# Transformer layer on one core: x's loads and the six-ahead weight pieces of the output projection begin earlier

## The chip, the cores and the metric

The kernel runs on one core of a Trainium2 chip. The metric is the device time of one execution in microseconds (us), as the median of several runs. Profiles and times by line come from one profiled execution.

## What is computed

The reference is one layer with sliding-window attention, for 512 tokens of width 2048, in float32:

```python
hn = rmsnorm(x, norm_g[0])
y = swa_mixer(hn, swa_w_in[0], swa_w_out[0], swa_sinks[0], rel_bias)   # attention, gated, times w_out
x = x + y
emb = p[0] @ ple_proj[0]
g = jax.nn.sigmoid(rmsnorm(x, ple_norm[0]) @ ple_gate[0])
x = x + emb * g
return rmsnorm(x, final_g)
```

The case is about the last product of `swa_mixer`, `(out * silu(gate)) @ w_out`, a 512 x 2048 by 2048 x 2048 product called the output projection here, and about `x + y`.

## The kernel before

**Stages.** The kernel projects x to queries, keys, values and gates, with the attention woven in (to about 452 us of the profile), then does the output projection, then the gate product with `ple_gate`, and at the end the last norm and the stores.

**Products in three.** Each float32 operand is split into a high and a low part, and TensorE makes three matmuls of one product (`mm3`, L123 to L128): high by high, high by low, low by high. ScalarE casts a raw weight piece to its high part (L700, named `bhi`); VectorE subtracts to get the low part (L701, `blo`).

**The output projection.** It is done as a Strassen scheme of seven half-size products with one of them replaced by smaller ones; the big products come in the order `ORDER_OUT = (1, 7, 6, 5, 3, 4)` (L623). Each has two halves `jj`, and each half four weight pieces `m` of 128 x 1024 float32, 512 KB. One piece feeds twelve matmuls of 128 x 512 in `unit` (L936 to L951). So product 1 has the pieces 0 to 7 of the stage, product 7 the pieces 8 to 15, product 6 the pieces 16 to 23. Smaller products' pieces come between those of the products 5, 3 and 4.

**Pieces and their rooms.** The class `Pieces` (L666 to L735) loads and splits them. `get(i)` is called ahead of piece i's matmuls and calls `ahead(i)` (L714 to L723), which issues the loads of pieces up to i+3, or up to i+6 for pieces between `far_from` and `far_to`, and then the splits up to piece i+2. A raw piece lies in one of three rooms (tag `wraw`, L692) or, between `far_from` and `far_to`, in one of eight (tag `grown`, L688). The eight rooms, like x's, lie in the pool `late` (L907), which takes the space of pools that the projections and the attention used and that are closed before the stage. The high and low parts have three rooms each. Before, `far_from` is the first piece of product 6, piece 16 (L778).

**x.** x is loaded in four parts of 512 columns, 1 MB each (`load_x`, L954 and L955), named by j. The finished sums of each product are added to or taken from x on VectorE (`add_to_x`, L989 to L997). `x_at` (L1070) says after which piece's matmuls a part's load stands in the program: the key is (product, half, piece). The sums of product 1's first half are held back until the first half of product 7, those of its second half until the first half of product 6 (`waiting`, L1071).

**Order on the engines.** In this stage TensorE's and SyncE's instructions keep the order of the program (`manual_schedule`, L63). All loads of pieces and of x are issued by SyncE, in one queue in that order: an instruction that waits for its room holds back all those behind it. The order of VectorE, ScalarE and POOL in this stage is chosen by the framework's planner by its own costs, from what is ready; in the attention and from the gate product's second Strassen product on it is written by hand as well.

Of the kernel before, what the change touches and what calls it, by code (L numbers as in the profile page):

```python
# [55 lines left out]
def trunk_kernel(ctx: ExitStack, tc: tile.TileContext, a: dict):  # L56
# [566 lines left out]
    ORDER_OUT, ORDER_PLE = (1, 7, 6, 5, 3, 4), (2, 7, 1, 6, 5, 3, 4)  # L623
# [115 lines left out]
    def add_stage(nm, order):  # L739
        at = {}  # L740

        def add_embeds(p, jj):
            if nm == "ple_gate" and p in (1, 5, 3, 4):
                j = jj + 2 * (p in (5, 3))
                B.add("proj", a["ple_proj"].rearrange("(k p) d -> p k d", p=P)[:, :, j * 512 : (j + 1) * 512])

        for p in order:
            for jj in range(2):
                if nm == "ple_gate" and (p, jj) == (4, 0):
                    for v in range(2):  # L750
                        at["e", v] = len(B.specs)
                        add_embeds(p, v)
                at[p, jj] = []
                for m in range(4):
                    at[p, jj].append(len(B.specs))
                    if (nm, p) in SUMS:
                        src = summed[nm, p, jj, m]
                    else:
                        src = block(nm, *{1: (1, 1), 2: (2, 1), 3: (2, 2), 6: (1, 1), 4: (2, 1)}[p], jj, m)
                    growing = () if nm == "w_out" else (7, 6, 4)  # L760
                    kind = "one" if p not in growing else "seed" if p == growing[0] else "grow"
                    B.add(kind, src, (nm, jj, m) if p in growing else None)
                    q = SMALL.get((p, jj), {}).get(m) if nm == "w_out" else None
                    if q is not None:
                        v = at.setdefault(("small", q), [])
                        src = summed.get(("small", q, len(v)))
                        if src is None:
                            src = small_block(*{1: (1, 1), 2: (2, 1), 3: (2, 2)}[q], len(v))
                        v.append(len(B.specs))
                        B.add("one", src)  # L770
                if p != 4:
                    add_embeds(p, jj)
        return at

    at_out = add_stage("w_out", ORDER_OUT)
    at_ple = add_stage("ple_gate", ORDER_PLE)

    far_from, far_to = at_out[6, 0][0], at_ple[ORDER_PLE[0], 0][0]  # L778

    class Forms:  # L780

# [285 lines left out]

    turns = []

    x_at = {(1, 1, 1): 0, (7, 0, 0): 2, (7, 0, 3): 1, (7, 1, 1): 3}  # L1070
    waiting = {(7, 0): (1, 0), (6, 0): (1, 1)}  # L1071
    held = {}
    for n, p in enumerate(ORDER_OUT):
# [344 lines left out]
```

## Time and profile before

| | us |
|---|---|
| median of 3 runs | 795.78 |
| the three runs | 794.87, 795.78, 796.67 |
| profiled execution | 794.62 |
| its span, first to last instruction | 792.9 |
| TensorE busy in the span | 782.9 |
| VectorE busy | 600.3 |
| ScalarE busy | 507.1 |
| output projection begins (first matmul with `bhi`) | 451.76 |

A row of a timeline has the start, the duration, the engine (PE is TensorE, DVE VectorE, ACT ScalarE, POOL GpSimd, SP SyncE, whose queue of instructions is SPq), the line, the operation and, in brackets, the idle time before it and what ended it. A row of waits has who waited, for whom, the sum in us, how often, and the longest. A row of the table by stretch has the stretch, its length, each engine's busy time (PE, PEld, DVE, ACT, POOL) with its count of instructions, the granted TensorE clock, the share of the DMA engines that was busy, and GB/s. A row of a load has its size and the median time from issue to landing.

### The profile page before, as it was taken

To read this page: it belongs to the slowest core of one execution; us is meant where nothing else is said; L and a number is where in the kernel's file an instruction comes from. 1 tells how busy PE (TensorE), PEld (TensorE's weight loads), DVE (VectorE), ACT (ScalarE), POOL (GpSimd) and SP (SyncE) were. 2 spreads that over 40 slices of the span, in tenths; PEclk is the share of its full clock that TensorE was granted. 3 is DMA by queue.
4 is the path that set the end of the run, shared out by engine and by line. 5 is a ranking of instruction groups with operands and counts; after the bars stand their busy time and mean duration, and the time that the engine had idled before them with its cause. 6 is when DMAs were issued, how large, how long until landed. Compare 5 with 4: busy or idle time off the path is not lost.

```text
span 792.9 us, 11070 instructions
## 1 busy us (share of the span) xinstructions
PE 782.9 (99%) x3746; PEld 655.1 (83%) x3746; DVE 600.3 (76%) x1043; ACT 507.1 (64%) x1066; POOL 122.2 (15%) x246
## 2 busy tenths in 40 slices
PE   9999999999999999999999999999999999999995
PEld 8888888888888888888888888888888888888885
DVE  4546697877878687877777899778867757988896
ACT  6742576666767586666666654466698656656765
POOL 0020223131323213132222100000000120200000
PEclk9999999999999999999999999999999999999998
DMA  9883499899999989998997369767764995787633
GB/s 352 281 212 132 116 271 316 243 277 235 278 257 267 250 254 272 228 280 238 260 259 187 107 236 393 300 210 235 275 236 140 347 206 195 160 226 216 182 107 106
DMA packets 45577, 185.22 MB, mean 234 GB/s; under 512 B 6656, under 2 KB 7680, under 8 KB 40400
## 3 DMA queue, kind: packets, MB, share of 16 engines
q1 hardware_dynamic: 37984, 145.40, 52.2%
q0 software_dynamic: 7536, 39.12, 26.1%
q8 instruction: 29, 0.48, 0.3%
q14 instruction: 28, 0.23, 0.1%
HBM read 177.63 MB, written 62.97 MB: 303 GB/s over the span
## 4 chain that ended last, share of the span: by engine, by line
PE 91%; DVE 4%; DMA 2%; ACT 1%; issue 1%; ACTq 0%; SPq 0%; DVEq 0%
PE qps L126 7%; PE qps L128 7%; PE qps L127 7%; PE gps L126 7%; PE gps L128 7%; PE gps L127 7%; PE g L126 5%; PE g L127 5%; PE g L128 5%; PE o L127 4%; PE o L126 4%; PE o L128 4%; PE s L462 2%; PE vps L279 2%; DVE blo L701 2%; PE o L557 2%
## 5 line engine op out<-in xcount | busy, mean ns | idle before, releaser
L701 DVE TENSOR_TENSOR blo<-braw,bhi 128x1024 fp32r<-128x1024 f32 x102 | 124.3, 1221 | 40.9 <-ACT bhi L700 40.6
L700 ACT CAST bhi<-braw 128x1024 fp32r<-128x1024 f32 x102 | 107.1, 1051 | 70.0 <-PE o L128 23.6
L126 PE MATMUL gps<-xh,whi 128*128 128x512 f32 x256 | 99.8, 390 | 0.1
L128 PE MATMUL gps<-xh,wlo 128*128 128x512 f32 x256 | 99.9, 390 | 0.0
L127 PE MATMUL gps<-xl,whi 128*128 128x512 f32 x256 | 99.8, 390 | 0.0
L126 PE MATMUL qps<-xh,whi 128*128 128x512 f32 x224 | 87.7, 391 | 0.0
L128 PE MATMUL qps<-xh,wlo 128*128 128x512 f32 x224 | 87.5, 390 | 0.0
L127 PE MATMUL qps<-xl,whi 128*128 128x512 f32 x224 | 87.3, 390 | 0.0
L110 DVE TENSOR_TENSOR wlo<-wraw,whi 128x1024 fp32r<-128x1024 f32 x60 | 73.8, 1232 | 2.9 <-ACT whi L109 2.5
L126 PE MATMUL g<-bhi,fhg 128*128 128x512 f32 x192 | 75.1, 391 | 0.0
L127 PE MATMUL o<-blo,fho 128*128 128x512 f32 x192 | 74.8, 390 | 0.2 <-DVE blo L701 0.2
L126 PE MATMUL o<-bhi,fho 128*128 128x512 f32 x192 | 74.8, 390 | 0.0
L128 PE MATMUL g<-bhi,flg 128*128 128x512 f32 x192 | 74.8, 389 | 0.0
L128 PE MATMUL o<-bhi,flo 128*128 128x512 f32 x192 | 74.7, 389 | 0.0
L127 PE MATMUL g<-blo,fhg 128*128 128x512 f32 x192 | 74.7, 389 | 0.0
L531 POOL TENSOR_SCALAR_AFFINE_SELECT own<-r 64x512 fp32r<-64x512 f32 (+1 forms) x48 | 32.5, 677 | 245.6 <-DVE r L521 245.6
L520 ACT CAST r<-pt 128x256 fp32r<-128x256 f32 x64 | 23.8, 371 | 71.7 <-PE pt L515 71.3
L521 DVE TENSOR_TENSOR r<-pt,r 128x256 fp32r<-128x256 f32 x64 | 27.1, 424 | 55.8 <-ACT r L520 54.9
L109 ACT CAST whi<-wraw 128x1024 fp32r<-128x1024 f32 x60 | 62.3, 1040 | 5.4 <-issue 3.9
L128 PEld LDWEIGHTS gps<-xh,wlo 128*128 128x128 f32 x256 | 48.0, 188 | 10.1
L126 PEld LDWEIGHTS gps<-xh,whi 128*128 128x128 f32 x256 | 48.1, 188 | 9.4 <-PE vps L279 0.5
L495 ACT ACTIVATE t<-t,sm 128x129 f32<-128x129 f32 x128 | 50.6, 397 | 8.0 <-DVE sm L491 6.4
(224 smaller groups left out, 1740.8 us busy)
## 6 DMA issues: line engine op xcount, KB each, us to landing
wraw<-in_w_gate_in SPq DMA_DIRECT2D x32, 512.0 KB, 6.9
w_out<-in_w_out POOLq DMA_DIRECT2D x32, 512.0 KB, 8.6
braw<-w_out SPq DMA_DIRECT2D x32, 512.0 KB, 4.6
wraw<-in_w_q SPq DMA_DIRECT2D x28, 512.0 KB, 6.3
braw<-in_ple_gate SPq DMA_DIRECT2D x24, 512.0 KB, 3.4
braw<-in_w_out SPq DMA_DIRECT2D x22, 512.0 KB, 4.3
xw<-in_first SPq DMA_DIRECT2D x14, 640.5 KB, 6.3
w_out<-in_w_out SPq DMA_DIRECT2D x16, 512.0 KB, 8.5
```

The source lines that it names most:

```text
L109: nc.scalar.copy(hi, raw)
L110: nc.vector.tensor_sub(lo, raw, hi.bitcast(F32))
L126: nc.tensor.matmul(ps, sh, mh, start=first, stop=False, skip_group_check=more)
L127: nc.tensor.matmul(ps, sh, ml, start=False, stop=False, skip_group_check=more)
L128: nc.tensor.matmul(ps, sl, mh, start=False, stop=last, skip_group_check=more)
L279: nc.tensor.matmul(v_ps[t], h[:, c], both[:, :, 256:512], start=f, stop=e, skip_group_check=True)
L495: nc.scalar.activation(su, su, AF.Exp, bias=sm[:, u : u + 1], accum_out=sm[:, 2 + u : 3 + u])
L520: nc.scalar.copy(rh, src)
L521: nc.vector.tensor_sub(rl, src, rh.bitcast(F32))
L531: nc.gpsimd.affine_select(out=flat(own), in_=flat(r).bitcast(F32), pattern=[[0, 8], [sign, HB]], compare_op=ALU.is_ge, fill=0.0, base=-HB ...
L700: nc.scalar.copy(hi, raw)
L701: nc.vector.tensor_sub(lo, raw, hi.bitcast(F32))
```

## The change

Two tables are changed, and nothing else. The first moves the point from which raw pieces use the eight rooms and are issued up to six pieces ahead, from piece 16 to piece 10 (the third piece of product 7's first half). The second moves x's four loads to earlier places in the program: part 0 from behind piece 5's matmuls to behind piece 3's, part 2 from 8 to 5, part 1 from 11 to 7, part 3 from 13 to 9.

```diff
-    far_from, far_to = at_out[6, 0][0], at_ple[ORDER_PLE[0], 0][0]
+    far_from, far_to = at_out[7, 0][2], at_ple[ORDER_PLE[0], 0][0]
...
-    x_at = {(1, 1, 1): 0, (7, 0, 0): 2, (7, 0, 3): 1, (7, 1, 1): 3}
+    x_at = {(1, 0, 3): 0, (1, 1, 1): 2, (1, 1, 3): 1, (7, 0, 1): 3}
```

With it the loads of the pieces 10 and on stand in the program ahead of those of 8 and 9: at piece 4 the program issues 7 and 10, at piece 5 it issues 8 and 11, at piece 6 it issues 9 and 12.

## The prediction

> **What bounds the kernel now.** First the page's engine line, then TensorE's waits.
>
> ```profile
> PE 782.9 (99%) x3746; PEld 655.1 (83%) x3746; DVE 600.3 (76%) x1043; ACT 507.1 (64%) x1066; POOL 122.2 (15%) x246
> PE o L127 <- DVE blo L701: 0.2, 1, 0.2
> ```
>
> TensorE works for 99% of the span, and after its start it waits for a semaphore once, in the output projection, for the low part of a weight piece. What an edit of the loads can win here is that stop; what it can lose is open. The pitch of the matmuls tells the stop's size better than the wait does, since ends are modelled.
>
> ```profile
> 451.76 0.40 PE L126 MATMUL o<-bhi,fho 128*128 128x512 f32 x1
> ...
> 492.14 0.39 PE L127 MATMUL o<-blo,fho 128*128 128x512 f32 x1
> 492.36 0.39 PE L128 MATMUL o<-bhi,flo 128*128 128x512 f32 x1
> 492.59 0.39 PE L126 MATMUL o<-bhi,fho 128*128 128x512 f32 x1
> 493.14 0.50 PE L127 MATMUL o<-blo,fho 128*128 128x512 f32 x1 [0.16 <-DVE blo L701]
> 493.48 0.40 PE L128 MATMUL o<-bhi,flo 128*128 128x512 f32 x1
> ```
>
> Matmuls start 0.227 us apart; twelve make a piece, 2.72 us. Two steps here are longer: 0.55 and 0.34 us, so 0.32 + 0.11 = **0.43 us** are lost. Piece 0 starts at 451.76, so 492.59 = 451.76 + 15 x 2.72 is the start of piece 15 (pieces are numbered from the projection's first). The chain of waits says why it was late:
>
> ```profile
> 483.02 7.68 DMA braw<-w_out
> 490.77 1.06 ACT bhi L700
> 491.86 1.24 DVE blo L701
> 493.14 0.50 PE o L127
> ```
>
> Its load left SyncE at 483.02 and took 7.68 us, then cast, subtraction, matmul. Why 7.68: SyncE's instructions in order, and the busy shares by stretch (the last two columns are DMA share and GB/s).
>
> ```profile
> 458.91 2.06 SPq L693 DMA_DIRECT2D braw<-in_w_out  x2
> 463.52 0.33 SPq L693 DMA_DIRECT2D braw<-w_out  x1
> 463.89 0.43 SPq L955 DMA_DIRECT2D x1s<-in_x  x1
> 466.92 6.60 SPq L693 DMA_DIRECT2D braw<-w_out  x3
> 473.57 0.43 SPq L955 DMA_DIRECT2D x1s<-in_x  x1
> 475.54 6.54 SPq L693 DMA_DIRECT2D braw<-w_out  x5
> 482.13 0.43 SPq L955 DMA_DIRECT2D x1s<-in_x  x1
> 483.02 1.39 SPq L693 DMA_DIRECT2D braw<-w_out  x3
> 484.46 0.44 SPq L955 DMA_DIRECT2D x1s<-in_x  x1
> 459.00:463.50 4.50, 4.50 (x21) 3.72 (x21) 4.50 (x6) 1.69 (x2) 0.00 (x0) 1.00 0.68 228
> 463.50:475.00 11.50, 11.50 (x53) 9.51 (x52) 10.52 (x12) 6.53 (x9) 0.00 (x0) 1.00 0.67 248
> 475.00:505.00 30.00, 29.84 (x132) 24.40 (x131) 26.00 (x31) 13.78 (x16) 0.00 (x0) 1.00 1.01 397
> 490.00:500.00 10.00, 9.84 (x44) 7.83 (x43) 8.97 (x12) 6.57 (x8) 0.00 (x0) 1.00 1.03 417
> 480.00:485.00 5.00, 5.00 (x24) 4.14 (x23) 3.61 (x5) 2.11 (x2) 0.00 (x0) 1.00 0.99 373
> ```
>
> The pieces by these rows, with the code's order: 6 and 7 (from 458.91), 8 (463.52), x0, 9, 10, 11, x2, then 12, 13, 16, 14, 17, then x1, 15, 18, 19, x3. From 475 to 505 the DMA engines are full at 397 GB/s; before, a third idle. Piece 15 stood behind x1, which is 1 MB. POOL has no instruction in any of these stretches, so its queue plays no part.
>
> VectorE is the second tight engine: 10.52 of 11.50 us. Its rows around the pieces 8 to 11, and what it stops for:
>
> ```profile
> 471.35 0.69 DVE L994 TENSOR_TENSOR x1s<-x1s,o 128x512 f32<-128x512 f32 x1 [0.98 <-DMA x1s<-in_x]
> 471.96 1.22 DVE L701 TENSOR_TENSOR blo<-braw,bhi 128x1024 fp32r<-128x1024 f32 x1
> 474.29 1.22 DVE L701 TENSOR_TENSOR blo<-braw,bhi 128x1024 fp32r<-128x1024 f32 x1
> 477.17 1.22 DVE L701 TENSOR_TENSOR blo<-braw,bhi 128x1024 fp32r<-128x1024 f32 x1
> 480.04 1.22 DVE L701 TENSOR_TENSOR blo<-braw,bhi 128x1024 fp32r<-128x1024 f32 x1
> ```
>
> Piece n is due at its second matmul, 451.76 + 2.72n + 0.23. So 9 (ready 475.51, due 476.50) has 0.99 us to spare, 10 (478.39, 479.22) 0.83 and 11 (481.26, 481.94) 0.68.
>
> **The change part by part.** It adds and removes no instruction: the same four loads of x (0.43 us of SyncE each) and the same pieces (0.33 us). What changes is their order on SyncE, and that the pieces 10 to 15 take one of eight rooms instead of one of three. In the three, piece n waits for the subtraction of n-3; in the eight, the first eight wait for nothing and 18 waits for the subtraction of 10. By the code the order becomes 6, x0, 7, 10, 8, 11, x2, 9, 12, 13, x1, 14, 15, x3, 16, 17, 18.
>
> *Issue.* 6 at 458.91 and 7 at 460.65 as before (7 waits for the subtraction of 4), x0 at about 459.3 between them, 10 right behind 7 (461.0), 8 at 463.52, 11 and x2 behind it (463.9, 464.2), 9 at 466.92 (behind the subtraction of 6), and 12 to 17 with x1 and x3 by about 470. So 15 leaves some 14 us sooner. It lands long before its cast, and **0.43 us go**. What is late next stands below.
>
> *The room under the loads.* x0 at 463.89 started straight behind 8, so the space was free by then; for 459.3 no row shows it. What lies there last belongs to the projections and the attention, whose matmuls end at 451.76 and whose last reader on VectorE is L584:
>
> ```profile
> 456.46 1.28 DVE L584 SCALAR_TENSOR_TENSOR gate<-gate,u 128x512 f32<-128x512 f32 x2
> SPq L693 <- DMA x1s<-in_x: 1.8, 1, 1.8
> ```
>
> That ends at 457.74, before 459.3, so I cost the wait at nothing; at most it is 463.89 - 459.3 = 4.6 us, in which 7 and all behind it stand still. The second row, of SyncE's own waits at 488 to 492, is a piece waiting for x1 to land, eight loads earlier in the order: only eight are under way at once. In the new order x1 waits for 7, x3 for 11, 16 for x2, all within a few us and none due before 484: nothing.
>
> *VectorE.* x0 lands before its addition, so the stop of 0.98 us at 471.35 goes and piece 9's subtraction could start at 473.3. No wait of TensorE hangs on that stop in this trace, so it gives 0 here, but it leaves slack.
>
> *Piece 9 is late next.* It stays in the three rooms, but now 10, 11 and x2 are ahead of it, with x0 and 7 and 8. How the queue serves them is seen in the times to landing (us, last column) of 6, 8, x0 and 9, with the cast of 9:
>
> ```profile
> braw<-in_w_out SPq DMA_DIRECT2D x1, 512.0 KB, 3.3
> braw<-w_out SPq DMA_DIRECT2D x1, 512.0 KB, 4.2
> x1s<-in_x SPq DMA_DIRECT2D x1, 1024.0 KB, 7.4
> braw<-w_out SPq DMA_DIRECT2D x1, 512.0 KB, 5.6
> 472.67 1.05 ACT L700 CAST bhi<-braw 128x1024 fp32r<-128x1024 f32 x1 [1.24 <-DMA braw<-w_out]
> ```
>
> 6 lands at 462.2; then the queue never runs empty. At 400 GB/s, nearest to the 397 of the full stretch, a piece takes 1.31 us and an x 2.62 us. Landing of 9: 462.2 + 2 x 2.62 (x0, x2) + 5 x 1.31 (7, 10, 8, 11, 9) = **474.0**, an estimate, against 466.92 + 5.6 = 472.5 before. The cast starts 0.2 us after the landing and is 1.05 us long, so the subtraction starts at 474.0 + 1.25 = 475.25, ends 476.47: just on time. But VectorE then stands 475.25 - 474.29 = 0.96 us behind its former times, and 11, with 0.68 us to spare, is late by **0.28 us**. Piece 8 lands at 468.7 by the same sum; it is needed by 471.3 (due 473.78, less 2.5): nothing.
>
> From the other side: 8 landed at 467.7, x0 at 471.3, 9 at 472.5, so x0 took 3.6 us there, not 2.6. With 3.6 for both x, 9 lands at 476.0. Below: 9 lands no later than 473.7 if its transfers run at the 417 GB/s of the fastest row (11.3 us in all), and then nothing is lost.
>
> Here the Trainium skill speaks against the change: "DMA: Bandwidth & Descriptors", section Specifications, gives a limit of about 358 GB/s for HBM per core. By that figure the transfers from x0 to 9, 4.72 MB, take 13.2 us, 9 lands at 475.4, and the net is a loss of 1.25 us (estimates). The trace does not agree: 397 GB/s held for 30 us.
>
> *Sum.* -0.43 + 0.28 = -0.15 us, on an execution of 794.62 us (span 792.9, 1.7 around it). The median of the three runs is 795.78, 1.16 above that execution, so the forecast is 795.78 - 0.15 = **795.6 us**. A difference of 0.2%, 1.6 us, is about what a measurement of this kernel can tell from no change.
>
> **The rivals.**
>
> *Piece 9 is held up (slower).* Both x take 3.6 us, 9 lands at 476.0, its subtraction starts at 477.25, VectorE is 2.96 us behind, piece 11 late by 2.28: 2.28 - 0.43 = +1.85, **797.6 us**. For: the measured x0. Against: x2, queued alone, and the full stretch ran at rate. It costs from a landing at 473.7 on, breaks even at 474.1, and passes 0.2% at 475.8. Chance 0.32, of it 0.25 over the bound.
>
> *A lower rate of the queue.* The lowest row of a full queue has 373 GB/s. At that the 4.72 MB from x0 to 9 take 12.65 us, 9 lands at 474.85, 11 is late by 0.28 + 0.85, and the net is +0.70, 796.5 us. For: the stretch is one of x and pieces mixed, as here. Against: its neighbours. Chance 0.05, same by the bound. (The Trainium skill's limit, quoted above from its DMA page, is this rival with a still lower rate.)
>
> *Ordinary runs lose more (faster).* The three runs are 1.16 us over the profiled one. If that is the same late landing of x0 and of 15, which the change removes, the gain is 0.43 + 1.16 = 1.6: **794.2 us**. For: VectorE's 0.98 us stop on x0 and 0.60 us of slack on piece 8 behind it. Against: nothing ties the 1.16 to this stage. Chance 0.18, 0.15 of it over the bound.
>
> *x0 must wait for its room*, up to 4.6 us, with 7 and 9 behind it: 9 lands at 478 or later, about 4 us lost, 799. Against: 457.74 above. Chance 0.05. ScalarE's and VectorE's order in this stage isn't written by hand and may come out otherwise; I add no sign for it.
>
> **How the numbers follow.** Forecast 0.40, same; with 0.05, 0.07 and 0.03 from the rivals same is 0.55; faster 0.15; slower 0.25 + 0.05 = 0.30. The range reaches from the full gain, 794.2, to a little over the held-up piece 9, 798.2; past it lie the waiting room and the worst landings.
>
> **What would show it.** Right: the stop at piece 15 is gone, no stop on x0 on VectorE, DMA share at 459 to 475 near 1, x0 issued near 459.3, and piece 9's landing at 474 with at most a few tenths lost at 9 to 11. Wrong: x0 issued after 460, piece 9 landing after 475.8, or a new stop of TensorE elsewhere in the projection.

## The result and the profile after

The changed kernel takes 798.45 us (median of ten runs, 797.01 to 800.75) against 796.29 for the kernel before (ten runs, 794.87 to 798.08): a ratio of 1.003, 95% interval 1.0016 to 1.0043. It is **slower**, by 1.3 to 3.4 us. The profiled execution took 798.36 us, its span is 796.7.

The engine line of the page of after, and its waits of TensorE (line and tile, what it waited for: us in total, times, longest us):

```profile
PE 783.2 (98%) x3746; PEld 655.3 (82%) x3746; DVE 600.6 (75%) x1043; ACT 507.4 (64%) x1066; POOL 124.4 (16%) x246
```

```profile
PE o L127 <- DVE blo L701: 1.9, 1, 1.9
PE o L559 <- ACT own L541: 1.6, 2, 1.5
```

TensorE is busy for 0.3 us more, while the span has grown by 3.8: the loss is idle time. The wait in the output projection has grown from 0.2 to 1.9 us. The second row is of the attention and is absent before; it is dealt with below.

TensorE's timeline of after, from the first matmul of the output projection to the first matmul of the gate product (tile `g`):

```profile
453.70 0.40 PE L126 MATMUL o<-bhi,fho 128*128 128x512 f32 x1
...
478.21 0.39 PE L126 MATMUL o<-bhi,fho 128*128 128x512 f32 x1
480.52 0.50 PE L127 MATMUL o<-blo,fho 128*128 128x512 f32 x1 [1.92 <-DVE blo L701]
480.86 0.39 PE L128 MATMUL o<-bhi,flo 128*128 128x512 f32 x1
...
611.21 0.48 PE L126 MATMUL g<-bhi,fhg 128*128 128x512 f32 x1
```

The same last matmul in before's timeline:

```profile
607.51 0.48 PE L126 MATMUL g<-bhi,fhg 128*128 128x512 f32 x1
```

478.21 is 453.70 + 9 x 2.72: the stop is at **piece 9**. Two steps of 2.31 and 0.34 us stand where 0.227 is usual, so 2.08 + 0.11 = 2.19 us are lost there. Piece 15 has no stop any more. The stage is 611.21 - 453.70 = 157.51 us long, before 607.51 - 451.76 = 155.75: 1.76 us more, which is 2.19 - 0.43. So every tenth of the stage's loss is at piece 9.

The stage also *starts* 1.94 us later in this profile. The instructions ahead of it stand in the same order in both kernels; what is later is the attention's wait at L559 (the row above). Below, that wait stands in the profiles of seven of the eight experiments too, also in ones whose loads differ from after's, and not in that of `far8`, whose stage starts at 451.87 although it has after's loads of x. `low9_thrice` has it with the loads of the kernel before, so it doesn't go with the loads; what brings it on isn't known. So stages are compared below by their own length, and whole kernels by ratios of many runs.

**The loads.** SyncE's instructions of after, in order:

```profile
461.24 0.43 SPq L955 DMA_DIRECT2D x1s<-in_x  x1
462.60 0.33 SPq L693 DMA_DIRECT2D braw<-in_w_out  x1
462.98 3.29 SPq L693 DMA_DIRECT2D braw<-w_out  x3
466.32 0.43 SPq L955 DMA_DIRECT2D x1s<-in_x  x1
468.87 1.27 SPq L693 DMA_DIRECT2D braw<-w_out  x3
```

Its DMA issues of after, piece 6 (issued at 460.86) and piece 9 (the first at 468.87), the last column being us to landing:

```profile
braw<-in_w_out SPq DMA_DIRECT2D x1, 512.0 KB, 3.7
braw<-w_out SPq DMA_DIRECT2D x1, 512.0 KB, 7.1
```

A stretch of after by engine (as in the prediction, the last columns are clock, DMA share, GB/s):

```profile
463.50:475.00 11.50, 11.50 (x52) 9.55 (x51) 11.50 (x13) 5.04 (x6) 0.00 (x0) 1.00 1.04 409
```

The order is 6, x0, 7, then 10, 8 and 11, x2, then 9, 12 and 13, as the code has it. x0 leaves at 461.24, which is 459.3 in before's time (1.94 earlier). Piece 9 lands at 468.87 + 7.1 = 475.97, 474.03 in before's time. From the landing of 6 near 464.6 to that of 9 the queue moved 4.72 MB in 11.4 us, 414 GB/s; the stretch above has 409, with the DMA engines full (1.04); from 459 to 463.5 they aren't yet (0.46).

**VectorE.** Its timeline of after, from the low part of piece 8 to that of piece 9:

```profile
473.44 1.21 DVE L701 TENSOR_TENSOR blo<-braw,bhi 128x1024 fp32r<-128x1024 f32 x1
474.57 0.68 DVE L818 TENSOR_TENSOR flo<-gate,fho 128x512 fp32r<-128x512 f32 x1
475.17 1.22 DVE L805 TENSOR_TENSOR gate<-gate,gate 128x1024 f32<-128x1024 f32 x1
476.31 0.68 DVE L1017 TENSOR_TENSOR small_sums<-gate 128x512 f32<-128x512 f32 x1
476.91 0.68 DVE L818 TENSOR_TENSOR flo<-gate,fho 128x512 fp32r<-128x512 f32 x1
477.51 0.68 DVE L1017 TENSOR_TENSOR small_sums<-gate,gate 128x512 f32<-128x512 f32 x1
478.11 1.21 DVE L805 TENSOR_TENSOR gate<-gate,gate 128x1024 f32<-128x1024 f32 x1
479.25 3.49 DVE L701 TENSOR_TENSOR blo<-braw,bhi 128x1024 fp32r<-128x1024 f32 x3
```

ScalarE's timeline of after, the casts of the pieces 9 and 10 in one row:

```profile
476.08 2.00 ACT L700 CAST bhi<-braw 128x1024 fp32r<-128x1024 f32 x2
```

Piece 9's cast ends near 477.1, so its low part could run from there to 478.35, and it is due at 478.44 (478.21 + 0.23). Instead it starts at 479.25. In between run four subtractions that prepare operands of product 3 (L805) and of the smaller products (L1017), all needed tens of us later, and one L818 subtraction, the low part of another operand. In before's timeline of VectorE the same four stand one behind the low part of 9 (474.29), two behind that of 10 (477.17) and one behind that of 11 (480.04):

```profile
475.43 1.22 DVE L805 TENSOR_TENSOR gate<-gate,gate 128x1024 f32<-128x1024 f32 x1
478.30 0.68 DVE L1017 TENSOR_TENSOR small_sums<-gate 128x512 f32<-128x512 f32 x1
478.90 1.22 DVE L805 TENSOR_TENSOR gate<-gate,gate 128x1024 f32<-128x1024 f32 x1
481.17 0.68 DVE L1017 TENSOR_TENSOR small_sums<-gate,gate 128x512 f32<-128x512 f32 x1
```

So the traces offer two stories.

- **Theory, the order:** the planner has put four subtractions ahead of piece 9's low part, and that alone costs the 2.19 us. The data came just in time.
- **Rival, the landing:** piece 9 lands too late (475.97, some 1.5 us later against its stage than before), and the four fill a gap that was there anyway.

### The profile page after: what moved, and what is told of

It is laid out like the page before. It is cut to its first block, busy times and chain, and to the rows that moved or that the text cites. A ratio compares the mean times of both kernels' runs of the same rounds, so it can differ in the third digit from the quotient of the medians.

```text
span 796.7 us, 11068 instructions
## 1 busy us (share of the span) xinstructions
PE 783.2 (98%) x3746; PEld 655.3 (82%) x3746; DVE 600.6 (75%) x1043; ACT 507.4 (64%) x1066; POOL 124.4 (16%) x246
## 4 chain that ended last, share of the span: by engine, by line
PE 94%; DMA 2%; DVE 2%; ACT 1%; issue 1%; ACTq 0%; DVEq 0%
PE qps L126 7%; PE qps L128 7%; PE qps L127 7%; PE gps L126 7%; PE gps L128 7%; PE gps L127 7%; PE g L127 5%; PE g L126 5%; PE g L128 5%; PE o L127 5%; PE o L126 5%; PE o L128 5%; PE s L462 2%; PE vps L279 2%; DMA wraw<-in_w_q 2%; PE o L557 2%
```

## The experiments

Each kernel is the changed one with the edit shown, unless before is named. The "stage" is from the first matmul of the output projection to the first of the gate product, "9 lands" is counted from the stage's start, and a loss is read from the matmuls' pitch as above. Ratios are to the kernel before.

| kernel | stage us | 9 lands after us | lost in the stage us, at piece | ratio (95%) |
|---|---|---|---|---|
| before | 155.75 | 20.8 | 0.43 at 15 | 1 |
| after | 157.51 | 22.3 | 2.19 at 9 | 1.003 (1.0016 to 1.0043) |
| low9_first | 155.35 | 22.3 | 0.04 | 1.0005 (0.9994 to 1.0017) |
| x_only | 156.84 | 20.7 | 1.08 at 11, 0.34 at 13 | 1.0019 (1.0007 to 1.0031) |
| far_only | 155.29 | 21.3 | 0 | 0.9998 (0.9983 to 1.0013) |
| far8 | 156.02 | 11.8 | 0.68 at 7 | 1.0007 (0.9992 to 1.0022) |
| low9_late | 159.35 | 24.6 | 2.40 at 9, 1.6 behind it | 1.0048 (1.0032 to 1.0065) |
| low9_thrice | 159.65 | 19.4 | 2.65 at 9, 1.7 behind it | 1.0049 (1.0027 to 1.0071) |
| x2_behind_9 | 155.27 | 19.8 | 0 | 1.0003 (0.9988 to 1.0018) |
| x_low11_first | 156.11 | 20.6 | 0.35 at 13, 0.42 at 14 | 1.0006 (0.9991 to 1.0022) |

**low9_first: only VectorE's order is put back.** The four subtractions are held behind piece 9's low part (`B.lows[i]` keeps the instruction that makes piece i's); the loads stay as in after.

```diff
+    def behind_low(i):
+        return tc.issue_after(B.lows[i].ins)
...
-                    nc.vector.tensor_sub(src, *sub)
+                    with behind_low(9) if self.nm == "o" and p == 3 else ExitStack():
+                        nc.vector.tensor_sub(src, *sub)
...
-            nc.vector.tensor_sub(src, *sub)
+            with behind_low(9):
+                nc.vector.tensor_sub(src, *sub)
```

> Loads as in the changed kernel; on VectorE alone four subtractions needed much later (two for product 3's forms, L805, two for the small products, L1017) are queued behind piece 9's low part. Theory (order): piece 9 lands as in the changed kernel, about 22.2 us after the stage's first matmul, its low part starts by 23.6 us instead of 25.5, and the 2.2 us that TensorE loses at piece 9 fall to 0.0 to 0.4; the time comes to 0.999 to 1.001 of before. Rival (landing): piece 9's data are what is late, the stop stays at 1.5 us or more and the time at 1.002 to 1.004.

VectorE's timeline of low9_first at the low parts 9, 10 and 11 (the first row) and the first subtraction held behind them (here L810 is after's L805):

```profile
477.42 3.64 DVE L701 TENSOR_TENSOR blo<-braw,bhi 128x1024 fp32r<-128x1024 f32 x3 [0.27 <-ACT bhi L700]
480.98 1.22 DVE L810 TENSOR_TENSOR gate<-gate,gate 128x1024 f32<-128x1024 f32 x1
```

TensorE's timeline of low9_first, the first two matmuls of piece 9:

```profile
478.55 0.39 PE L126 MATMUL o<-bhi,fho 128*128 128x512 f32 x1
478.77 0.43 PE L127 MATMUL o<-blo,fho 128*128 128x512 f32 x1
```

Piece 9 lands as late against the stage as in after (22.3 us), VectorE now even stands still for its cast (0.27 us), and yet the second matmul comes 0.22 us behind the first: next to nothing is lost (0.04 us, at the third). The 2.19 us are the order's. The landing is just in time.

**x_only and far_only: each half of the change alone.**

```diff
 # x_only
-    far_from, far_to = at_out[7, 0][2], at_ple[ORDER_PLE[0], 0][0]
+    far_from, far_to = at_out[6, 0][0], at_ple[ORDER_PLE[0], 0][0]
 # far_only
-    x_at = {(1, 0, 3): 0, (1, 1, 1): 2, (1, 1, 3): 1, (7, 0, 1): 3}
+    x_at = {(1, 1, 1): 0, (7, 0, 0): 2, (7, 0, 3): 1, (7, 1, 1): 3}
```

> Only x's four loads are moved; the rooms and the distance of the pieces stay. Order of issue 6, x0, 7, 8, x2, 9, 10, x1, 11. Theory (order): piece 9 has one room's worth less ahead of it and lands at about 19.6 us after the stage's start, VectorE meets it in its turn; no stop over 0.2 us, and the 0.43 us at piece 15 go too; 0.999 to 1.0005 of before. Rival (the x loads ahead of the pieces are what costs): a stop of over 1 us at one of the pieces 7 to 11, 1.002 or more.

> Only the pieces 10 to 15 get the eight rooms and the distance of six; x's loads stay. Order of issue 6, 7, 10, 8, 11, x0, 9, 12. Theory (order): piece 9 lands at about 20.8 us after the stage's start, with x0 alone ahead of it; stop of 0 to 0.4 us, time 0.999 to 1.001. Rival (two pieces issued ahead of 9 are enough to make it late): over 1 us at piece 9, 1.002 or more.

`far_only` did as expected: no stop of the stage is left, neither at 9 nor at 15. It is the change without its fault, and gains the 0.43 us of piece 15 in its stage (155.29 against 155.75), which the ratio can't tell from nothing.

`x_only` did not: I expected no stop. TensorE's timeline of x_only at piece 11:

```profile
484.82 0.39 PE L126 MATMUL o<-bhi,fho 128*128 128x512 f32 x1
486.03 0.50 PE L127 MATMUL o<-blo,fho 128*128 128x512 f32 x1 [0.82 <-DVE blo L701]
```

0.98 us go there, and 0.10 at the next step. VectorE's timeline of x_only ahead of piece 11's low part:

```profile
482.95 1.28 DVE L994 TENSOR_TENSOR x1s<-x1s,o 128x512 f32<-128x512 f32 x2
484.15 0.68 DVE L1017 TENSOR_TENSOR small_sums<-gate,gate 128x512 f32<-128x512 f32 x1
484.75 2.35 DVE L701 TENSOR_TENSOR blo<-braw,bhi 128x1024 fp32r<-128x1024 f32 x2
```

And ScalarE's timeline of x_only, the casts of 11 and 12 with the wait ahead of them:

```profile
482.85 2.26 ACT L700 CAST bhi<-braw 128x1024 fp32r<-128x1024 f32 x2 [2.80 <-DMA braw<-w_out]
```

With x1 put ahead of it and only three rooms, 11 lands near 482.8 and its cast ends near 483.9. Two updates of x (L994) are then under way, and one of the L1017 subtractions still goes first. Had the low part started at 483.9, it would have ended at 485.1 (with 1.22 us); started behind the updates, at 484.15, it would have ended at 485.3 or a little later. It is due at 485.05 (484.82 + 0.23). So by this arithmetic 0.1 to 0.3 of the 1.08 us are the landing's and the rest the order's. The 0.34 us at piece 13 are no landing's: its cast (488.34, 1.05 us) ends at 489.4, two updates of x (L992, L994) go first, and the low part starts at 490.58; started at 489.4 it would have ended at 490.6, a full 1 us before it is due.

**x_low11_first: x_only with VectorE's order pinned at piece 11.** The L1017 subtractions, the second L805 one of product 3 and the additions to x behind the unit (1, 1) are held behind low part 11 in the same way.

```diff
...
+            with behind_low(11):
+                nc.vector.tensor_sub(src, *sub)
...
+            with behind_low(11) if (p, jj) == (1, 1) else ExitStack():
+                add_to_x(j, t, sign, ps)
```

> x's loads alone moved, and on VectorE the small products' subtractions, product 3's second and the two additions of x's part 1 are queued behind piece 11's low part. If the order on VectorE made the stop at 11: it falls from 1.08 us to 0.1 to 0.4; what is lost at 13, 0.34 us, hangs on the landing and stays or grows. If the landing of 11 made it: it stays near 1 us.

The stop at 11 is gone and the stage is 0.73 us shorter. But this doesn't settle x_only's split: ScalarE's timeline of x_low11_first has 11's cast as follows.

```profile
482.53 1.05 ACT L700 CAST bhi<-braw 128x1024 fp32r<-128x1024 f32 x1 [2.59 <-DMA braw<-w_out]
```

The stage starts at 456.61 here and at 454.87 in x_only. So the cast comes 25.9 us after the start, in x_only 28.0: the piece landed 2 us earlier behind the same loads. With that landing the order may not have mattered. The 2 us stand already in the load of piece 10, which takes 6.5 us to landing in x_only and 4.3 here; what makes that difference wasn't found. The stop at 13 stays, as expected, but not for the reason given there, and one at 14 is new. Both are the order's again, by the same arithmetic: 13's cast ends at 490.2, updates of x go first, and its low part starts at 491.19; 14's cast ends at 493.5, and an L810 subtraction (after's L805, at 493.23) goes first, so its low part starts at 494.36.

**far8: the eight rooms from two pieces earlier.**

```diff
-    far_from, far_to = at_out[7, 0][2], at_ple[ORDER_PLE[0], 0][0]
+    far_from, far_to = at_out[7, 0][0], at_ple[ORDER_PLE[0], 0][0]
```

> The changed kernel, but with the eight rooms and the distance of six from piece 8 on, so that 8 and 9 are issued ahead of x0. Both theories: piece 9 lands by about 14 us after the stage's start, no stop at 9, none at 15; 0.9985 to 1.0005 of before. If the eight rooms are not free so early, SyncE stands still at piece 8 and piece 6 or 7 is late instead, over 1 us.

The stop at 9 is gone, and that at 15, but a new one stands in TensorE's timeline of far8:

```profile
470.94 0.39 PE L126 MATMUL o<-bhi,fho 128*128 128x512 f32 x1
471.74 0.50 PE L127 MATMUL o<-blo,fho 128*128 128x512 f32 x1 [0.42 <-DVE blo L701]
```

It is at piece 7 (451.87 + 7 x 2.72): 0.57 us, and 0.11 at the next step, 0.68 in all. That piece's DMA issue in far8 (the last column is us to landing):

```profile
braw<-in_w_out SPq DMA_DIRECT2D x1, 512.0 KB, 7.9
```

And its cast in ScalarE's timeline of far8 (one row with the next piece's):

```profile
468.73 2.00 ACT L700 CAST bhi<-braw 128x1024 fp32r<-128x1024 f32 x2
```

VectorE's timeline of far8 at the low part of piece 7 (the second row, with the next one's):

```profile
469.87 0.69 DVE L818 TENSOR_TENSOR flo<-gate,fho 128x512 fp32r<-128x512 f32 x1
470.47 2.35 DVE L701 TENSOR_TENSOR blo<-braw,bhi 128x1024 fp32r<-128x1024 f32 x2
```

Issued at 460.77, 7 lands at 468.7, behind 8, 9 and x0; the cast starts with the landing and ends near 469.8. The last piece in the three rooms lands late again, but it isn't the landing alone that stops TensorE: an L818 subtraction goes first. Had the low part started in its place, at 469.87, it would have ended at 471.09, and it is due at 471.17 (470.94 + 0.23). So by this arithmetic the landing takes all the room but 0.1 us, as at piece 9 in after, and the order does the rest; no run pins the order here.

**low9_late: how late may piece 9 land?** low9_first with the load of 9 issued behind those of 12 and 13.

```diff
-            for n in range(max(i, 0), min(i + 6, last) + 1):
+            for n in sorted(range(max(i, 0), min(i + 6, last) + 1), key=lambda n: n == 9 and i == 7):
+                if n == 9 and i == 6:
+                    continue
```

> The kernel with piece 9's low part ahead on VectorE (no stop at 9), and piece 9's load now issued behind those of 12 and 13, so that two more pieces, 2.6 us, are ahead of it. If landing counts once the order is right: 9 lands about 24.9 us after the stage's start, its low part ends at 27.3, due at 24.7, and TensorE stops for about 2.6 us; the time 1.002 to 1.005 of before. If the order of VectorE is all that counts: no stop, as in the run before.

TensorE's timeline of low9_late, the last matmul of piece 8 and the first two of piece 9:

```profile
478.11 0.39 PE L128 MATMUL o<-bhi,flo 128*128 128x512 f32 x1
479.61 0.50 PE L126 MATMUL o<-bhi,fho 128*128 128x512 f32 x1 [1.10 <-ACT bhi L700]
480.87 0.50 PE L127 MATMUL o<-blo,fho 128*128 128x512 f32 x1 [0.76 <-DVE blo L701]
```

Landing 2.3 us later costs a stop of 1.27 + 1.03 us, and 0.10 at the next step, 2.40 in all, with VectorE's order pinned. So the landing is a real limit: 24.6 us is past it, and after's 22.3 is just short of it, as the 0.04 us of low9_first show.

**low9_thrice: the data in time, VectorE late.** The kernel before, with piece 9's subtraction done three times over (the same result each time).

```diff
-            nc.vector.tensor_sub(lo, raw, hi.bitcast(F32))
+            for _ in range(3 if i == 9 else 1):
+                nc.vector.tensor_sub(lo, raw, hi.bitcast(F32))
```

> The kernel before, with piece 9's subtraction on VectorE done three times into the same place (the last is the one that TensorE waits for; the planner puts another subtraction and piece 10's between them). Loads as before, 9 lands at 20.7 us after the stage's start. If a late VectorE alone stops TensorE with the data there in time: the third ends about 28.3 us after the start, due 24.7, stop of 3 to 4 us, 1.003 to 1.005 of before. If VectorE has slack to take it in: under 1 us.

TensorE's timeline of low9_thrice:

```profile
478.43 0.39 PE L126 MATMUL o<-bhi,fho 128*128 128x512 f32 x1
481.20 0.50 PE L127 MATMUL o<-blo,fho 128*128 128x512 f32 x1 [2.39 <-DVE blo L702]
```

With before's loads, the first of the three subtractions ends at 476.6, 2 us before it is due. The two repeats, with an L806 subtraction (before's L805) and piece 10's low part between them, 4.5 us in all, move the end of the last to 481.15. TensorE stops for 2.54 us, and 0.11 at the next step, 2.65 in all, less than the 3 to 4 expected. The stop has after's form. The whole loss is larger than the stop; that is told at the end.

**x2_behind_9: the change with x2 one piece later,** so that 9 is issued ahead of it.

```diff
-    x_at = {(1, 0, 3): 0, (1, 1, 1): 2, (1, 1, 3): 1, (7, 0, 1): 3}
+    x_at = {(1, 0, 3): 0, (1, 1, 2): 2, (1, 1, 3): 1, (7, 0, 1): 3}
```

> The changed kernel with part 2 of x one piece later, behind piece 9 and 12 in the queue. Piece 9 has one x less ahead of it and lands about 19.6 us after the stage's start; the planner then puts its low part ahead of product 3's and the small products' subtractions by itself. No stop over 0.2 us in the projection; the stage takes 155.3 us from its first matmul to the next stage's first, as where nothing is lost; 0.999 to 1.001 of before. If issuing 10 and 11 ahead of 9 is what costs, the stop of 2 us stays.

VectorE's timeline of x2_behind_9:

```profile
474.98 1.22 DVE L805 TENSOR_TENSOR gate<-gate,gate 128x1024 f32<-128x1024 f32 x1
476.11 1.21 DVE L701 TENSOR_TENSOR blo<-braw,bhi 128x1024 fp32r<-128x1024 f32 x1
```

Only one L805 subtraction stands ahead of 9's low part now, and nothing is lost. Nothing pins the order here: moving one 1 MB load behind one more piece's matmuls was enough for the planner to put three of the four subtractions back behind it. That fits a planner that reckons piece 9 to land too late in after, and so fills VectorE; its own costs weren't seen, so this reason is argued and not shown.

No version beats the kernel before by more than the measurement can tell: far_only, x2_behind_9 and low9_first gain at most 0.5 us in the stage.

## Why the prediction was wrong, step by step

- **The stop at piece 15 goes, -0.43 us:** right.
- **x0 issued at 459.3, no wait for its room, no stop of VectorE on x0:** right (461.24 - 1.94).
- **Piece 9 lands at 474.0 by 400 GB/s:** right (474.03); that it is so exact is luck, since two errors cancel: 6 landed 0.4 us later than reckoned, and the queue then took 11.4 us instead of 11.8 (414 GB/s). The rival with both x at 3.6 us (476.0) is wrong, and so is the one with 373 GB/s: 409 GB/s held for 11.5 us. The Trainium skill's limit of about 358 GB/s ("DMA: Bandwidth & Descriptors", section Specifications), which is one of two cores' share of a memory stack there, isn't borne out by that row either; this program runs on one core. The first rival's 797.6 us is near the result, but by another mechanism.
- **"VectorE then stands 0.96 us behind its former times, and 11 ... is late by 0.28 us":** this step failed. It takes before's *order* of VectorE as given and moves its times. The four subtractions behind the low parts of 9, 10 and 11 were rows of before's trace, with a planner free to move them; I wrote that the order "may come out otherwise; I add no sign for it", and so put this term at nothing without a price. It came out otherwise: the four went ahead of 9's low part, 11 lost nothing, and in place of the 0.28 us stand 2.19 us at piece 9. low9_first takes away the order alone, with the same landing, and the loss falls to 0.04.
- **The sum:** -0.43 + 2.19 = +1.76 us in the stage, as measured (157.51 - 155.75). The medians differ by 2.16, whose interval of 1.3 to 3.4 us holds it.
- **The base:** the forecast stood on 795.78, the median of three runs; ten give 796.29.
- **The 1.16 us between profile and median** were no sign of this stage: `far_only` loses nothing in it, and its time is still that of before (0.9998, at the least 0.9983, where a gain of 0.43 + 1.16 us would be 0.998). The waits at L559 in the attention, 1.0 to 2.2 us in all, stand in most profiles and not in before's; that they make up the 1.16 us fits, but isn't shown.

One thing was right that the sum hid: 9's landing had no room left. In low9_first its low part starts at 477.42, and with 1.22 us it is ready at 478.64, for a matmul at 478.77.

## What to carry to other kernels

Where a planner orders an engine, moving a load also moves that engine's work: list the instructions that are ready and not urgent beside each tight one, and price the case that all of them go first (here 3.5 us of subtractions against a slack of 0.1; that is a bound, and 2.19 us were lost, since part of them ran before the piece was there). Then either pin the urgent ones first or choose the place of the load so that the planner needn't fill a gap. And ask of each group of shared rooms which piece is the last in it: its load is held until the rooms empty, while all that was moved ahead lands before it (9 here, 7 in far8). A late landing then takes the slack, and the order on VectorE decides whether TensorE stops.

## What the runs showed of the hardware

**A stop of about 2.5 us can cost some 4 us.** The same stretch, right behind the stop, of low9_late and of after (the third column from the end is TensorE's granted clock):

```profile
481.20:485.00 3.80, 3.80 (x11) 2.98 (x10) 3.80 (x5) 0.25 (x1) 0.00 (x0) 0.55 1.03 410
```

```profile
481.20:485.00 3.80, 3.80 (x19) 3.11 (x18) 2.10 (x3) 1.05 (x1) 0.00 (x0) 1.00 1.03 410
```

In low9_late, as in low9_thrice (there at a clock of 0.65), TensorE does 11 matmuls where after does 19. Two such matmuls of low9_thrice's timeline:

```profile
482.55 0.63 PE L126 MATMUL o<-bhi,fho 128*128 128x512 f32 x1
482.97 0.63 PE L127 MATMUL o<-blo,fho 128*128 128x512 f32 x1
```

They start 0.42 us apart instead of 0.227. With the stops of 2.40 and 2.65 us the two stages are 4.0 and 4.35 us longer than those without a loss (159.35 and 159.65 against some 155.3), so 1.6 to 1.7 us are the clock's. The mean granted clock of an execution tells whether it happened in others: it is 0.994 in both profiles, as in six of low9_late's eight runs and in four of low9_thrice's five. In x_low11_first it followed a shorter stop, a wait of 1.7 us at L559 in the attention. The stretch right behind that, of x_low11_first, has a clock of 0.61:

```profile
130.00:134.00 4.00, 4.00 (x13) 3.15 (x12) 3.48 (x10) 3.55 (x11) 2.44 (x4) 0.61 1.03 319
```

After's stop at piece 9, a wait of 1.92 us and 2.19 by the pitch, had none of it in the profiled execution (0.998). Three of after's ten runs have a mean clock of 0.994, though, at 798.5 to 800.75 us (of the 58 runs of the kernel before that were timed beside the experiments, one has it); whether the stop at piece 9 or a wait in the attention brought it on there isn't seen, and the part of it in the 2.16 us between the medians is open. The Trainium skill ("TensorE: Matmul & The Clock Gate", section "Part 1: The HAM clock gate (the "warmup" mystery)") tells of half clock after one idle window of about 3.4 us that runs freely. Here stops well under that length sufficed, some of the time, so the rule doesn't hold here as it stands. That some do and others don't may hang on where a stop falls against such a window; no run here varied that.
